# Six of 22 feed-forward convolutions in the down stage, other engines for the weight sums, and a new order at both ends of the up stage

## The chip, the cores and the metric

One core of a Trainium2 chip runs the whole program. The metric is device time in microseconds (us) from launch to end, the median of a few runs. PE is TensorE, DVE is VectorE, ACT is ScalarE, POOL is GpSimd, SP is SyncE (here it only issues DMAs).

## The reference

One layer of a diffusion trunk on 1152 tokens (128 context, 1024 latent on a 16 x 64 grid), width 1024. The part that matters is its second half, after the two token mixers:

```
h = rmsnorm(x, norm_g[2]) * (1 + sc2) + sh2
u_act, u_val = split(h @ ffn_up, 2)               # 1024 -> 2 x 2816
u_act = dwconv_grid(u_act, ffn_conv, rows) + ffn_conv_b   # 3x3 per channel
f = (silu(u_act) * u_val) @ ffn_down              # 2816 -> 1024
x = x + g2 * rmsnorm(f, norm_g[3])
```

On the grid the convolution is 3 x 3, on the 128 context tokens it has width 3. Everything is float32.

## The kernel before

A float32 matrix product is done as three reduced-precision products: an operand is split into a high part (a copy on ACT) and a low part (the difference, on DVE), and high x high, high x low and low x high are summed in PSUM. The program is one long stream for each engine. A scheduler places the instructions; where `pe.on` is set, PE keeps the order in which the code is written, and the other engines' queues are filled by the scheduler.

- **Output projection** (`wo_mm`, line 1499): nine blocks of 128 tokens. Behind each block come two norms (lines 1513 to 1525) and `modulate` (line 1466): eight transposes on PE, scale and shift on ACT and DVE, and a DMA of the normed tokens `hf` to DRAM (`h2d`). `mod_cols` computes one of eight column groups of the last gate behind each block from the second on.
- **Up stage.** The 2816 channels are 22 blocks of 128, each with an activation and a value half. The product of one block with 1152 tokens is done by Strassen's scheme in the Winograd form: the tokens are halved (c = 0, 1), and seven products P1 to P7 of sums of operand quarters take the place of eight. One product for one half of the tokens is a unit: 12 matmuls of 288 columns (line 70), so 14 units and 168 matmuls a block, 308 units in all. `w_split` (line 1614) makes the seven weight operands: ACT copies the high part (line 1622), DVE (for P5 and P3 POOL) subtracts for the low part (line 1623), and POOL forms four sums (lines 1626 to 1630). The token operands `T1` to `T4` come from `x_rest` and `x_late`.
- A unit ends in PSUM (`pu`, eight banks in a ring) and is taken out by `unit` (line 1638): P1 and P2 by ACT, then for P2 a sum on POOL (line 1658), the others by DVE (lines 1660 to 1669), into `uraw` (activation) and `uval` (value).
- `conv` (line 1671) runs one block behind: ACT writes bias and centre tap to `ua` (line 1675), DVE adds eight taps on the grid (line 47) and two on the context (line 50), ACT applies SiLU (line 1679), POOL multiplies with `uval` (line 1680) and POOL's queue sends the block to DRAM (`f2d`).
- **Down stage.** Three sweeps of three token blocks, each over k = 0 to 21. `f_group` reads `f2d` back in groups of eight k and splits it into `fg` (ACT line 1695, DVE line 1696). `wd_split` loads a row block of the down weights and splits it (ACT line 1706, DVE line 1707); `NS` = 13 of these are loaded again in each sweep, nine stay (`wr`). A sweep runs its first k over all its blocks, and the last k block by block, with the closing norm of each block behind it.

## Time and profile before

| what | value |
|---|---|
| median of three runs | 2302.42 us (2297.89 to 2305.01) |
| time of the profiled execution | 2297.62 us |
| its span, first to last instruction | 2295.9 us |
| mean granted TensorE clock | 0.961 of 2.4 GHz |
| PE / DVE / ACT / POOL busy | 90% / 65% / 38% / 37% |

In the chain of work that ended last PE has 43% of the span, DVE 27% and DMA 12%. The share of busy time is a mean over stages of very different kinds; the stretches that the change touches lie from about 1400 us on. Durations of POOL are rough, and a matmul's duration overlaps the next one's, so that matmuls are counted here from start to start.

### The profile page before, as it was taken

To read this page: it belongs to the slowest core of one execution; us is meant where nothing else is said; L and a number is where in the kernel's file an instruction comes from. 1 tells how busy PE (TensorE), PEld (TensorE's weight loads), DVE (VectorE), ACT (ScalarE), POOL (GpSimd) and SP (SyncE) were. 2 spreads that over 40 slices of the span, in tenths; PEclk is the share of its full clock that TensorE was granted. 3 is DMA by queue.
4 is the path that set the end of the run, shared out by engine and by line. 5 is a ranking of instruction groups with operands and counts; after the bars stand their busy time and mean duration, and the time that the engine had idled before them with its cause. 6 is when DMAs were issued, how large, how long until landed. Compare 5 with 4: busy or idle time off the path is not lost.

```text
span 2295.9 us, 41348 instructions
## 1 busy us (share of the span) xinstructions
PE 2062.2 (90%) x16579; PEld 1876.9 (82%) x16579; DVE 1498.9 (65%) x2219; ACT 878.6 (38%) x1702; POOL 856.5 (37%) x916
## 2 busy tenths in 40 slices
PE   5999998988999998888799997899899989779998
PEld 4998998977988887788789776888888888667787
DVE  4666779788555567545533445999999999935332
ACT  3663646362234333355311334323322322324231
POOL 2000288888432333445122011555655565200000
PEclk9999999989999999999999998999999999899999
DMA  9144444444845555467657565211221121356351
GB/s 260 52 104 113 126 126 115 130 113 120 211 109 145 137 136 140 147 201 231 227 173 244 191 191 133 67 58 58 77 68 58 58 76 59 126 182 223 121 175 46
DMA packets 401583, 305.80 MB, mean 133 GB/s; under 512 B 92369, under 2 KB 369269, under 8 KB 401392
## 3 DMA queue, kind: packets, MB, share of 16 engines
...
HBM read 220.15 MB, written 82.94 MB: 132 GB/s over the span
## 4 chain that ended last, share of the span: by engine, by line
PE 43%; DVE 27%; DMA 12%; issue 9%; ACT 6%; POOL 1%; SPq 1%; DVEq 0%; ACTq 0%; POOLq 0%
PE pg L398 10%; PE pfd L70 10%; DVE ua L47 8%; PE pwo L1499 4%; PE pbr L70 4%; PE pg L70 4%; PE pu L70 2%; DVE ua L50 2%; PE pY L70 1%; ACT ua L1675 1%; DMA aw<-in_ada_w 1%; SPq L76 1%; DMA wraw<-in_ffn_down 1%; PE pmN L70 1%; DMA bon<-bond 1%
## 5 line engine op out<-in xcount | busy, mean ns | idle before, releaser
L398 PE MATMUL pg<-act,whi 128*128 128x384 f32 (+1 forms) x1696 | 329.6, 342 | 0.9 <-DVE act L361 0.4
L70 PE MATMUL pu<-x,hl 128*128 128x288 f32 x2024 | 299.9, 298 | 30.0 <-DVE uraw L1667 27.3
L70 PEld LDWEIGHTS pu<-x,hl 128*128 128x128 f32 x2024 | 277.1, 189 | 39.1 <-issue 31.6
L398 PEld LDWEIGHTS pg<-act,whi 128*128 128x128 f32 (+1 forms) x1696 | 297.5, 189 | 7.8 <-DVE act L361 0.8
L47 DVE SCALAR_TENSOR_TENSOR ua<-uraw,par,ua 128x945 f32<-128x945 f32 (+2 forms) x176 | 253.4, 1440 | 30.9 <-ACT ua L1675 29.6
L70 PE MATMUL pu<-xb,hl 128*128 128x288 f32 x1672 | 252.1, 298 | 20.1 <-DVE uval L1662 9.1
L70 PEld LDWEIGHTS pu<-xb,hl 128*128 128x128 f32 x1672 | 231.0, 190 | 29.6 <-DVE uval L1662 13.5
L398 PE MATMUL pg<-act,wlo 128*128 128x384 f32 (+1 forms) x848 | 168.7, 338 | 8.4 <-DVE wlo L385 8.4
L70 PE MATMUL pfd<-whi,fg 128*128 128x512 f32 x468 | 150.2, 403 | 23.6 <-ACT whi L1706 13.0
L398 PEld LDWEIGHTS pg<-act,wlo 128*128 128x128 f32 (+1 forms) x848 | 147.9, 186 | 12.1 <-DVE wlo L385 8.7
L1622 ACT ACTIVATE hl<-wraw 128x512 fp32r<-128x512 f32 x132 | 79.0, 630 | 194.5 <-POOL wraw L1628 175.9
L1623 DVE TENSOR_TENSOR hl<-wraw,hl 128x512 fp32r<-128x512 f32 x110 | 135.6, 1233 | 16.6 <-ACT hl L1622 16.4
L385 DVE TENSOR_TENSOR wlo<-wraw,whi 128x1024 fp32r<-128x1024 f32 (+1 forms) x64 | 80.9, 1267 | 99.0 <-ACT whi L384 98.8
L543 POOL TENSOR_TENSOR tmp<-La,Lb 96x31 f32<-96x31 f32 (+15 forms) x155 | 124.8, 805 | 28.9 <-DMA La<-Ad 17.1
L545 POOL TENSOR_TENSOR Lb<-Lb,tmp 96x31 f32<-96x31 f32 (+15 forms) x155 | 126.8, 818 | 12.2
L70 PEld LDWEIGHTS pfd<-whi,fg 128*128 128x128 f32 x468 | 90.8, 195 | 45.2 <-ACT whi L1706 15.1
L70 PE MATMUL pfd<-wr,fg 128*128 128x512 f32 x486 | 110.6, 389 | 0.0
...
L70 PEld LDWEIGHTS pfd<-wr,fg 128*128 128x128 f32 x486 | 91.2, 188 | 18.9
L1707 DVE TENSOR_TENSOR wlo<-wraw,whi 128x1024 fp32r<-128x1024 f32 x39 | 48.0, 1231 | 87.2 <-ACT whi L1706 87.2
L70 PE MATMUL pg<-act,whi 128*128 128x384 f32 x496 | 103.3, 360 | 0.0
L1680 POOL TENSOR_TENSOR uval<-uval,ua 128x1152 f32<-128x1152 f32 x22 | 61.5, 2795 | 103.9 <-ACT ua L1679 103.9
...
## 6 DMA issues: line engine op xcount, KB each, us to landing
...
f2d<-uval POOLq DMA_DIRECT2D x22, 576.0 KB, 3.1
...
sgz<-zraw ACTq DMA_DIRECT2D x16, 576.0 KB
...
```

The costliest lines, as they stand in the source:

```text
L47: v.scalar_tensor_tensor(o, img[:, r0 + i:r1 + i, c0 + j:c1 + j], wt, o, op0=ALU.mult, op1=ALU.add)
L50: v.scalar_tensor_tensor(o, raw[:, max(0, j):128 - max(0, -j)], wt, o, op0=ALU.mult, op1=ALU.add)
L70: return (lambda *a, **k: tc.keep_in_program_order(f(*a, **k))) if self.on else f
L385: v.tensor_tensor(lo, raw, hi.bitcast(F32), op=ALU.subtract)
L398: pe.matmul(out, wt(hw, k), at(ha, k), start=(i == 0), stop=(i == last))
L543: e.tensor_tensor(t3, L[:, j, i].unsqueeze(2).to_broadcast([NI, n, m]), X[:, j:j + 1, c].to_broadcast([NI, n, m]), op=ALU.mult)
L545: e.tensor_tensor(X[:, i, c], X[:, i, c], t3, op=ALU.subtract)
L1499: pe.matmul(pts[b][q], AS[g][:, ha, k, 128 * o:128 * o + 128], wo2[k][hw][:, 0, 512 * q:512 * q + 512], start=(k == 0 and i == 0), stop=(k ...
L1622: s.activation(w[:, 0], src, AF.Copy)
L1623: (gp if m in ("P5", "P3") else v).tensor_tensor(w[:, 1], src, f32(w[:, 0]), op=ALU.subtract)
L1680: gp.tensor_tensor(val, val, ua, op=ALU.mult)
L1707: v.tensor_tensor(lo, raw, f32(hi), op=ALU.subtract)
```

## The change

- **Late convolutions.** Blocks 1, 5, 9, 13, 17 and 21 (`LATE`) have no convolution in the up stage. `put_off` sends their `uraw` and `uval` to DRAM (`latd`, on SP's queue). In the first down sweep `late_convs` loads them and runs the same convolution from new tiles (`lraw`, `lval` two each, `lua` one), three or four steps for each k. `KO` puts these six blocks at k = 16 to 21.
- **Engines.** The sum behind P2 is done by DVE straight from PSUM. All seven low parts are on DVE. Of the four weight sums two stay on POOL and two go to DVE, all four at P6.
- **Down sweeps** of 4, 3 and 2 token blocks; 15 weight blocks are loaded again in each sweep and seven stay; `f_group` has six k instead of eight.
- **Order.** `modulate` of the last token block stands behind the fourth unit, in the up products; the four first units are P1 and P2 of blocks 0 and 1 for the first half of the tokens; `x_rest(0)` and the loads of the second half stand behind it (`x_mid`, `x_late`). `mod_cols` stands behind blocks 0 to 7 instead of 1 to 8.

```
+    LATE = (1, 5, 9, 13, 17, 21)
+    KO = [i for i in range(NFB) if i not in LATE] + list(LATE)
-        (gp if m in ("P5", "P3") else v).tensor_tensor(w[:, 1], src, f32(w[:, 0]), op=ALU.subtract)
+        v.tensor_tensor(w[:, 1], src, f32(w[:, 0]), op=ALU.subtract)
-        if m == "P1":
-            gp.tensor_tensor(s1, a21, a22, op=ALU.add)
-            gp.tensor_tensor(a21, a11, a21, op=ALU.subtract)
-            gp.tensor_tensor(a11, s1, a11, op=ALU.subtract)
-        if m == "P2":
-            gp.tensor_tensor(a12, a12, a11, op=ALU.subtract)
+            gp.tensor_tensor(s1s[i], a21, a22, op=ALU.add)
+            gp.tensor_tensor(a21, a11, a21, op=ALU.subtract)
+            v.tensor_tensor(a11, s1s[i], a11, op=ALU.subtract)
+            v.tensor_tensor(a12, a12, a11, op=ALU.subtract)
...
-                s.activation(act[:, t1], pt, AF.Copy)
-                gp.tensor_tensor(act[:, t1], act[:, t1], act[:, t2], op=ALU.add)
+                v.tensor_tensor(act[:, t1], pt, act[:, t2], op=ALU.add)
...
+        def put_off(i):
+            dma(latd[LATE.index(i), 0], acts.pop(i))
+            dma(latd[LATE.index(i), 1], vals.pop(i))
+            yield
+        SWEEPS = ((0, 4), (4, 3), (7, 2))
-        NS = 13
+        NS = 15
...
+            if u == 4:
+                modulate(ob, NB - 1)
+                x_mid()
...
-                conving = conv(i)
+                conving = (put_off if i in LATE else conv)(i)
...
+        def late_convs():
+            for j, i in enumerate(LATE):
+                raw, val = (fo.tile([128, T], F32, name=nm, tag=nm) for nm in ("lraw", "lval"))
+                dma(raw, latd[j, 0])
+                dma(val, latd[j, 1])
+                yield from conv_of(i, raw, val, fd.tile([128, T], F32, name="lua", tag="lua"))
...
+                for _ in range(3 + k % 2):
+                    next(late, None)
```

PE's queue behind the last product of the output projection, before (`ptx` are transposes, `pmod` and `pmt` belong to `mod_cols`, `pu` are units):

```order
L1499 MATMUL pwo<-whi,act_164 128x512
L1473 MATMUL ptx<-ident,ob 128x128 [waits DVE_49,Activation_49]
L1473 MATMUL ptx<-ident,ob 128x128 x3
L1473 MATMUL ptx<-ident,ob 128x128 [waits PE_49]
L1473 MATMUL ptx<-ident,ob 128x128 x3
L258 MATMUL pmod<-aw,sc 32x128 [waits DMAHW3_49,Activation_49]
L258 MATMUL pmod<-aw,sc 32x128 x7
L267 MATMUL pmt<-sel,mrow 128x2 [waits Activation_49]
L70 MATMUL pu<-x_14216,hl 128x288 [waits DVE_49,Activation_49]
```

The same place of the same queue now:

```order
L1500 MATMUL pwo<-whi,act_165 128x512
L70 MATMUL pu<-x_14233,hl 128x288 [waits DVE_49]
L70 MATMUL pu<-x_14233,hl 128x288 x35
L70 MATMUL pu<-x_14233,hl 128x288 [waits Activation_49]
L70 MATMUL pu<-x_14233,hl 128x288 x7
L70 MATMUL pu<-x_14233,hl 128x288 [waits DVE_49]
L70 MATMUL pu<-x_14233,hl 128x288 x3
L70 MATMUL ptx<-ident,ob 128x128 [waits DVE_49]
L70 MATMUL ptx<-ident,ob 128x128 x7
L70 MATMUL pu<-xb_14545,hl 128x288 [waits Activation_49]
```

Four units (48 matmuls) have moved ahead of the transposes, and `mod_cols` is gone from between.

DVE's queue from the end of one up block into the next, before (`hl` are weight low parts, `ua` convolution taps, the rest takes units out of PSUM); every block reads like this:

```order
L1623 TENSOR_TENSOR hl<-wraw,hl 128x512 [waits Activation_49]
L1669 TENSOR_TENSOR uraw<-pu,uraw 128x288 [waits DVE_49,PE_49] x2
L47 SCALAR_TENSOR_TENSOR ua<-uraw,par,ua 128x15x63 [waits Activation_49]
L50 SCALAR_TENSOR_TENSOR ua<-uraw,par,ua 128x127
L47 SCALAR_TENSOR_TENSOR ua<-uraw,par,ua 128x960 [waits DVE_49]
L50 SCALAR_TENSOR_TENSOR ua<-uraw,par,ua 128x127 [waits DVE_49]
L47 SCALAR_TENSOR_TENSOR ua<-uraw,par,ua 128x15x63 [waits DVE_49]
L47 SCALAR_TENSOR_TENSOR ua<-uraw,par,ua 128x16x63 [waits DVE_49] x2
L1660 TENSOR_TENSOR uraw<-pu,uraw 128x288 [waits PE_49,Pool_49]
L1623 TENSOR_TENSOR hl<-wraw,hl 128x512 [waits DMAHW0_49,Activation_49]
```

The same place now, behind a late block (lines 1627 and 1628 are the two weight sums that came to DVE, line 1671 is the sum behind P2):

```order
L1682 TENSOR_TENSOR uraw<-pu,uraw 128x288 [waits DVE_49,PE_49]
L1633 TENSOR_TENSOR hl<-s_17934,hl 128x512 [waits Activation_49]
L1633 TENSOR_TENSOR hl<-wraw,hl 128x512 [waits PE_49,Activation_49]
L1671 TENSOR_TENSOR uraw<-pu,uraw 128x288 [waits PE_49] x2
L1633 TENSOR_TENSOR hl<-wraw,hl 128x512 [waits DMAHW0_49,Activation_49]
L1627 TENSOR_TENSOR wraw<-s_18169,wraw 128x512 [waits DVE_49,Pool_49]
L1673 TENSOR_TENSOR uraw<-pu,uraw 128x288 [waits PE_49] x2
L1633 TENSOR_TENSOR hl<-wraw,hl 128x512 [waits Activation_49]
L1628 TENSOR_TENSOR wraw<-wraw 128x512 [waits DVE_49]
```

The ten taps are gone from the block behind a late one; in the other blocks they stand between these rows as before.

ACT's queue in the first down sweep, now (`whi` and `fg` are copies of weights and of `f`, `lua` belongs to the late convolutions, line 1637 is its start and 1641 its SiLU); before, only rows like the first two kinds stood here:

```order
L1718 ACTIVATE whi<-wraw 128x1024 [waits DMAHW4_49,DVE_49,PE_49]
L1637 ACTIVATE lua<-lraw,par 128x1152 [waits DMASW4_49,DMASW5_49,DMASW3_49,DMASW6_49,DMASW2_49,DMASW7_49,DMASW1_49,DMAHW5_49,DMASW0_49,DMAHW7_49,DVE_49,Pool_49]
L1718 ACTIVATE whi<-wraw 128x1024 [waits DMAHW7_49,DVE_49,PE_49]
L1708 ACTIVATE fg<-fg 128x1024 [waits DMAHW0_49]
L1708 ACTIVATE fg<-fg 128x1024 [waits DMAHW1_49]
L1708 ACTIVATE fg<-fg 128x1024 [waits DMAHW2_49]
L1718 ACTIVATE whi<-wraw 128x1024 [waits DMAHW3_49,DVE_49,PE_49]
L1708 ACTIVATE fg<-fg 128x1024 [waits DMAHW6_49]
L1641 ACTIVATE lua<-lua 128x1152 [waits DVE_49,Activation_49]
L1718 ACTIVATE whi<-wraw 128x1024 [waits DMAHW0_49,PE_49,Activation_49]
L1637 ACTIVATE lua<-lraw,par 128x1152 [waits DMAHW4_49,Pool_49]
```

The second start of `lua` waits for POOL: there is one `lua`, and POOL's product of the convolution before it has to have read it.

## Rows read from the trace of the kernel before

**Rows 1.** Busy time of each engine by stretch (us from the span's start and length, then busy us and instructions of PE, PEld, DVE, ACT, POOL, the granted clock, the DMA share and GB/s): the head of the up stage, its steady part, the start and the rest of the down stage, the end.

```profile
1401.80:1461.20 59.40, 39.90 (x255) 37.89 (x255) 43.61 (x52) 27.69 (x47) 24.22 (x18) 0.77 0.41 94
1461.20:1982.50 521.30, 478.09 (x3470) 460.29 (x3468) 482.32 (x553) 152.00 (x262) 295.68 (x199) 1.00 0.20 64
1982.50:2102.50 120.00, 97.56 (x397) 77.30 (x397) 66.31 (x77) 48.29 (x58) 8.74 (x4) 0.90 0.57 193
2102.50:2289.90 187.40, 183.14 (x794) 149.19 (x792) 59.44 (x76) 46.22 (x69) 0.00 (x0) 0.99 0.39 133
2289.90:2295.90 6.00, 0.00 (x0) 0.00 (x0) 2.17 (x4) 0.97 (x3) 0.00 (x0) 0.68 0.23 87
```

**Rows 2.** Timeline of PE in the up stage (start, duration, engine, line, operation, count): two units that follow each other without a wait.

```profile
1462.82 1.74 PE L70 MATMUL pu<-x,hl 128*128 128x288 f32 x12
1464.40 1.75 PE L70 MATMUL pu<-xb,hl 128*128 128x288 f32 x12
```

**Rows 3.** What PE waited for in the steady up stage (total us, times, longest).

```profile
PE pu L70 <- DVE uraw L1667: 28.2, 19, 1.5
```

**Rows 4.** What DVE waited for in the same stretch.

```profile
DVE ua L47 <- ACT ua L1675: 29.0, 20, 2.0
```

**Rows 5.** Timeline of ACT, DVE and POOL around the end of one convolution and the start of the next.

```profile
1704.32 1.19 DVE L47 SCALAR_TENSOR_TENSOR ua<-uraw,par,ua 128x945 f32<-128x945 f32 x1
...
1705.60 1.17 ACT L1679 ACTIVATE ua<-ua 128x1152 f32<-128x1152 f32 x1 [3.91 <-DVE ua L47]
...
1706.85 2.69 POOL L1680 TENSOR_TENSOR uval<-uval,ua 128x1152 f32<-128x1152 f32 x1 [3.83 <-ACT ua L1679]
1707.32 2.77 DVE L1623 TENSOR_TENSOR hl<-wraw,hl 128x512 fp32r<-128x512 f32 x1 [0.48 <-ACT hl L1622]
...
1713.07 1.35 ACT L1675 ACTIVATE ua<-uraw,par 128x1152 f32<-128x1152 f32 x1 [4.74 <-DVE uraw L1669]
...
1714.45 1.38 DVE L47 SCALAR_TENSOR_TENSOR ua<-uraw,par,ua 128x945 f32<-128x945 f32 x1 [1.42 <-ACT ua L1675]
```

**Rows 6.** Groups of DVE's instructions in the steady up stage (count, busy us, mean ns of one, idle before).

```profile
L1623 DVE TENSOR_TENSOR hl<-wraw,hl 128x512 fp32r<-128x512 f32 x100 | 125.2, 1252 | 8.9 <-ACT hl L1622 8.9
...
L47 DVE SCALAR_TENSOR_TENSOR ua<-uraw,par,ua 128x960 f32<-128x960 f32 x42 | 79.8, 1900 | 0.0
...
L50 DVE SCALAR_TENSOR_TENSOR ua<-uraw,par,ua 128x127 f32<-128x127 f32 x42 | 44.0, 1047 | 0.0
```

**Rows 7.** Groups of POOL's instructions in the same stretch.

```profile
L1680 POOL TENSOR_TENSOR uval<-uval,ua 128x1152 f32<-128x1152 f32 x20 | 53.9, 2696 | 71.4 <-ACT ua L1679 71.4
...
L1627 POOL TENSOR_TENSOR wraw<-wraw 128x512 f32<-128x512 f32 x19 | 24.9, 1312 | 1.5
```

**Rows 8.** Timeline of DVE: single instructions of the kinds that an up block is made of, at a place where POOL holds none of them up.

```profile
1465.07 1.20 DVE L47 SCALAR_TENSOR_TENSOR ua<-uraw,par,ua 128x960 f32<-128x960 f32 x1
...
1466.20 0.44 DVE L1662 TENSOR_TENSOR uval<-pu,uraw 128x288 f32<-128x288 f32 x1
...
1466.57 0.67 DVE L1623 TENSOR_TENSOR hl<-wraw,hl 128x512 fp32r<-128x512 f32 x1
1467.17 1.19 DVE L47 SCALAR_TENSOR_TENSOR ua<-uraw,par,ua 128x945 f32<-128x945 f32 x1
...
1471.83 1.26 DVE L47 SCALAR_TENSOR_TENSOR ua<-uraw,par,ua 128x1008 f32<-128x1008 f32 x1
...
1473.01 0.34 DVE L50 SCALAR_TENSOR_TENSOR ua<-uraw,par,ua 128x127 f32<-128x127 f32 x1
```

**Rows 9.** Timeline of PE at the start of the up stage; in brackets the idle time ahead and what ended it.

```profile
1401.61 0.39 PE L1499 MATMUL pwo<-whi,act 128*128 128x512 f32 x1
1414.17 1.94 PE L1473 MATMUL ptx<-ident,ob 128*128 128x128 f32 x8 [12.17 <-DVE ob L1525]
...
1419.02 6.13 PE L70 MATMUL pu<-x,hl 128*128 128x288 f32 x24 [0.84 <-ACT hf L1481]
```

**Rows 10.** Timeline of PE from the up stage into the down stage, and three matmuls of the first sweep that follow each other without a wait.

```profile
1980.77 1.75 PE L70 MATMUL pu<-xb,hl 128*128 128x288 f32 x12
1991.13 0.79 PE L70 MATMUL pfd<-whi,fg 128*128 128x512 f32 x1 [8.62 <-ACT fg L1695]
1993.90 0.80 PE L70 MATMUL pfd<-whi,fg 128*128 128x512 f32 x1 [1.97 <-DVE fg L1696]
...
2026.57 1.22 PE L70 MATMUL pfd<-whi,fg 128*128 128x512 f32 x2 [9.04 <-ACT whi L1706]
...
2045.06 0.62 PE L70 MATMUL pfd<-whi,fg 128*128 128x512 f32 x2
...
2045.74 0.62 PE L70 MATMUL pfd<-whi,fg 128*128 128x512 f32 x2
```

**Rows 11.** What SP's queue waited for from 1960 us to the end (total us, times, longest).

```profile
SPq L76 <- POOL uval L1680: 11.3, 1, 11.3
```

**Rows 12.** Timeline at the start of the third down sweep: a weight load is issued, then split by ACT and DVE.

```profile
2209.93 13.04 SPq L76 DMA_DIRECT2D wraw<-in_ffn_down  x5
...
2214.19 1.06 ACT L1706 ACTIVATE whi<-wraw 128x1024 fp32r<-128x1024 f32 x1 [3.83 <-DMA wraw<-in_ffn_down]
2215.28 1.23 DVE L1707 TENSOR_TENSOR wlo<-wraw,whi 128x1024 fp32r<-128x1024 f32 x1 [3.67 <-ACT whi L1706]
```

**Rows 13.** DMA issues on the page: the finished blocks on their way to DRAM (KB each, us to landing).

```profile
f2d<-uval POOLq DMA_DIRECT2D x22, 576.0 KB, 3.1
```

More of the change, by code (lines that the diff above doesn't have):

```diff
@@ L1525, in _body @@
                 v.tensor_scalar(ob, xt, s2, None, op0=ALU.mult)
-                modulate(ob, b)
-                if b > 0:
-                    for _ in mod_cols(128 * (39 + b), 128, (8,), aw_, wt, pss):
+                if b < NB - 1:
+                    modulate(ob, b)
+                    for _ in mod_cols(128 * (40 + b), 128, (8,), aw_, wt, pss):
                         pass
@@ L1565, in x_rest, with x_mid @@
         x_split(c, "T4", td, his[3], r21)
-    x_rest(0, ta, tb, (r11, r12, r21, r22), [quarter(x2, i) for i in range(4)])
     q11, q12, q21, q22 = xb[4:8]
-    x_load(1, 0, 0, q11)
-    x_load(1, 1, 0, q21)
-    x_split(1, "X11", q11, xb[1], xb[2])
-    x_split(1, "X21", q21, xb[3], xb[8])
-    x_load(1, 0, 1, q12)
-    x_load(1, 1, 1, q22)
+    def x_mid():
+        x_load(1, 0, 0, q11)
+        x_load(1, 1, 0, q21)
+        x_split(1, "X11", q11, xb[1], xb[2])
+        x_split(1, "X21", q21, xb[3], xb[8])
+        x_rest(0, ta, tb, (r11, r12, r21, r22), [quarter(x2, i) for i in range(4)])
     def x_late():
+        x_load(1, 0, 1, q12)
+        x_load(1, 1, 1, q22)
         x_split(1, "X22", q22, xb[9], xb[10])
@@ L1777, in w_next @@
                 res[k] = wd_split(k, *(fd.tile([128, D], F32R, name=f"wr{x}{k}") for x in range(2)))
[L1779 to L1780 removed]
+        for sw, (b0, nb) in enumerate(SWEEPS):
+            pd = [[psg([128, 512], "pfd") for q in range(2)] for o in range(nb)]
             no = NFB - 3 if sw == 0 else NS
             for k in range(no):
[L1784 to L1786 removed]
+                if k in (2, 7):
+                    for _ in f_group(sw, (k + 4) // 5):
+                        pass
+                if k == 13:
+                    g3 = f_group(sw, 3)
+                    next(g3)
+                if k == no - 1:
+                    next(g3)
                 if k + 2 < NFB:
@@ L1789, in _body @@
                 w = wds.pop(k) if k < NS else res[k]
-                for o in range(3):
+                for o in range(nb):
                     for q in range(2):
                         down_mm(pd[o][q], sw, k, o, q, w, k == 0, False)
+                for _ in range(3 + k % 2):
+                    next(late, None)
+            for _ in late:
+                pass
             if sw == 0:
                 w_next(sw, NFB - 1)
-            for o in range(3):
-                b = 3 * sw + o
-                if o == 0 and sw < 2:
+            for o in range(nb):
+                b = b0 + o
+                if o == nb - 2 and sw < 2:
                     for _ in f_group(sw + 1, 0):
```

76 lines of the change are left out of this document (37 added, 39 removed).

## Prediction

> **What bounds the kernel now.** I read the busy time by stretch first, then who waits for whom in the up stage, then the timeline there, then both ends of the stage. The steady up stage takes 521.3 us for 3470 matmuls [rows 1]. A block has 168, so that is 20.65 blocks of 25.2 us. Two units that follow each other without a wait start 1.58 us apart [rows 2], so PE needs 14 x 1.58 = 22.2 us a block and stands 3 us. It waits for DVE to empty PSUM: 28.2 us in 19 waits, about one a block [rows 3]. DVE is busy 482 of 521 us, and most of the rest is the wait for ACT to begin a convolution, 29.0 us in 20 blocks [rows 4].
>
> But DVE's busy time is not work. Follow one place in the timeline [rows 5]: POOL's product runs from 1706.85 to 1709.54, a weight low part on DVE starts at 1707.32 and ends at 1710.09, 0.55 us behind it. Alone the same instruction takes 0.67 [rows 8], on the mean 1.25 [rows 6]; a 960-wide tap takes 1.20 alone and 1.90 on the mean, a context tap 0.34 and 1.05. So while POOL runs, a DVE instruction that reads two SBUF operands stands still. Instructions that take a unit out of PSUM are not held up. DVE's own work in a block, with the last 0.08 us of each duration under the next one, as the starts show [rows 8]: 5 low parts x 0.60 = 3.0; 12 PSUM reads x 0.37 = 4.4; taps 4 x 1.11 + 2 x 1.13 + 2 x 1.18 + 2 x 0.26 = 9.6 (the widths 945, 960, 1008, 127); sum 17.0. Busy is 482/20.65 = 23.4, so 6.4 us a block are held up by POOL, which is busy 295.7/20.65 = 14.3 us a block [rows 1]. The bound of the up stage is what DVE and POOL share, not DVE's arithmetic.
>
> **Steady up stage.** In a block with a convolution DVE now has 7 low parts (4.2), two weight sums priced as low parts of the same shape (1.2), 14 PSUM reads (5.2) and taps (9.6): 20.2 us. POOL keeps two weight sums (1.3 each) and the product (2.7): 5.3 us [rows 7]. With the wait for ACT, 0.8 us instead of 1.4 since a low part stands in it now, that is 21.0 us if POOL holds nothing up and 26.3 if it holds DVE up for all its length. At the old ratio (6.4 of 14.3) it is 23.4; I take 25.2, nearer the upper end, because there the product held DVE up for nearly its whole length [rows 5]. In a block behind a late one the taps and the product are gone: 10.6 us and some 2 us of POOL, 12.7.
>
> The row shows one such hold [rows 5]. The Trainium skill (SBUF — State Buffer, Who interferes with whom) makes it a rule: a VectorE instruction with two SBUF inputs and a GpSimd instruction that reads SBUF exclude each other for a whole instruction. By that rule alone POOL's 5.3 us count in full wherever DVE has no PSUM read in hand, which is rival (d), 2277 in place of 2260.
>
> Four blocks then need 3 x 25.2 + 12.7 = 88.3 us of DVE, against 4 x 22.2 = 88.8 us of PE. They tie, if DVE may fall behind by 3 us in each of three blocks and catch up in the fourth. It may: PE has eight banks, so it runs up to seven units (11 us) ahead, and the low parts stand seven or more units ahead of their use. Nine of eleven is tight, so I allow 0.6 us a block: 22.8 us. **Gain 20.65 x (25.2 - 22.8) = 50 us**, between 62 (PE's floor) and 10 (no catching up: (3 x 25.2 + 22.2)/4 = 24.4, and more if POOL holds more).
>
> The two stores of a late block go on SP's queue and wait for its last PSUM reads; queued behind them are weight loads for two blocks later, so nothing waits at once. I price them at 0.
>
> **Head of the up stage.** PE stood 12.2 us for the norm of the last token block [rows 9]. Four units, 6.3 us, now stand there. The chain of the norm itself keeps its length: in DVE's queue three low parts of operands, a difference and two PSUM reads stand between its steps, about as many as before. Also gone from PE's path are `mod_cols`, which had it from the end of the transposes at 1416.1 to 0.84 us ahead of 1419.02, and part of the slow clock: the 24 matmuls there took 6.13 us, 255 ns each [rows 9], twice the 132 ns of the steady stage [rows 2]; the mean granted clock of the stretch is 0.77, partly 1.2 and partly 2.4 GHz [rows 1]. What is late next: the operands T1 to T4 of the first half, six instructions of 1152 columns on DVE at 1.3 us (by their width, [rows 8]), stand largely behind the transposes now, and `x_late` needs the last tokens through DRAM. I expect PE to stand twice for 5 to 6 us. **Gain 9 us**, from 3 to 14.
>
> **Into the down stage.** PE stood 8.6 us, then 2.0, then ran at half speed, and stood 9.0 more at 2026.57 for a weight load [rows 10]. That load was queued on SP behind one that waited 11.3 us for the last convolution's product [rows 11]. Now the first groups of `f` are old blocks, but SP's second fetch stands behind the store of block 21, which waits for DVE, by then some 9 us behind PE. So the first wait stays near 10 to 13 us; the second goes.
>
> **First down sweep.** Two matmul pairs of it start 0.68 us apart with one more between [rows 10]: 0.227 us each. Four blocks are 528 matmuls, 119.7 us of PE. The late convolutions form a chain beside it. Between two of them: SiLU 1.2, POOL's product 2.7, the start on ACT 1.35 [rows 5] and some 0.3 of handover, 5.5 us, because there is one `lua`. Each has 9.6 us of taps, 58 in all; five gaps make 28. DVE's queue also has, between the taps of the six, 22 weight and `f` low parts of 0.9 to 1.15 [rows 12], 25 us. The first tap stands behind the weight part for k = 2, which waits for PE to finish k = 0: about 22 us after PE leaves the up stage. Behind the last tap come SiLU and product (4), the store (3.1 to landing [rows 13]), the fetch (4.3, as a weight load takes from issue to use [rows 12]) and the split (2.3): 14 us. So k = 20 and 21 are ready 22 + 58 + 28 + 25 + 14 = 147 us after the up stage, and PE, which could be there at 125, waits; then 69 matmuls, half of the first ones slow, take 19 us. **The sweep ends 167 us after the up stage**, between 140 (chain hidden) and 180.
>
> The one or two weight parts in each gap may stand under POOL's product as the one at 1707.32 did [rows 5], some 6 us in all; that is kept for the range.
>
> **Other sweeps.** The second has 396 matmuls, 90 us, and 1 us of switch. The third has 264, 60 us, but only 2.7 us a k. A weight load takes 4.3 us from issue to use and 2.3 us to split [rows 12], 6.6 for one of two buffers, 3.3 a k: 11 of the 15 loaded k cost 0.6 more, 6 us. At two blocks a sweep this is a new wait for DMA. So from the up stage's end to the last matmul 167 + 91 + 66 = 324 us, against 1982.5 to 2289.9 = 307.4 before [rows 1]. **Loss 17 us**, from a gain of 10 to a loss of 30. The 6 us behind the last matmul stay.
>
> **Sum.** -50 - 9 + 17 = -42 us on the profiled 2297.6; the median shown is 4.8 higher, so 2302.4 - 42, rounded to 2260.
>
> **Rivals.** (a) The chain of late convolutions hides behind PE, as its DVE work of some 100 us in 120 would allow: the sweep takes 140, the rest as above: 2233, at PE's floor in the up stage 2221. Against it stands the one `lua`. (b) The late blocks don't help, because three blocks in a row with a convolution already fill the banks: 24.4 to 25 us a block, gain 10 instead of 50: 2300. For it speaks that PE already waits for PSUM in every block [rows 3]. (c) Slower: weights, convolution inputs and `f` share SP's queue in the first sweep. An input two convolutions on waits for POOL's product, weights stand behind it, and taps stand behind their low parts on DVE. If the loop closes, each late convolution costs a load and a split more (4.3 + 2.3): 6 x 6.6 = 40 us. It decides from the point where a weight load is issued less than 6.6 us before its low part is due; by my times the margin is 1 to 8 us. With (b) it gives 2340, alone 2300. (d) POOL holds DVE up for all its 5.3 us: 26.3 us a block, 13.2 behind a late one, 92.1 us for four, 23.0 a block and 0.6 as above, gain 33 instead of 50: 2277. For it speaks the hold at 1707.32 [rows 5], against it that PSUM reads are a quarter of DVE's work and run beside POOL. With (b) this is 25.3 a block, no gain in the up stage at all, so the change would not do there what it says: 2311.
>
> **How the numbers follow.** Forecast (2240 to 2285) 0.50; (a) 0.15; (b) 0.13; (c) 0.10; (d) 0.12. The measurement can tell 0.3%, 7 us, from no change. Faster: forecast, (a), (d) and a small part of (b) and (c): 0.79; same 0.09; slower 0.12. The range 2228 to 2296 leaves out the lower end of (a) and most of (b) and (c).
>
> **What the next profile would show.** Right: blocks of 22 to 23.5 us in the up stage; low parts near 0.8 us on the mean instead of 1.25; POOL busy near 5 us a block; a wait of 15 to 30 us of PE in the first sweep before k = 20, ended by `fg`; weights awaited by ACT in the third. Wrong: PE still waiting for PSUM in every block, no wait in the first sweep, or many waits there for `whi` and `wlo` behind loads.

## The result and the profile after

The changed kernel takes 2265.72 us (median of four runs, 2261.67 to 2274.78) against 2302.61 us before (four runs too): a ratio of 0.9848, 95% interval 0.981 to 0.9885. 2260 was forecast, in a range of 2228 to 2296.

The profiled execution of the changed kernel is its slowest, 2274.78 us, and was slow ahead of everything that the change touches: the output projection begins at 1289.3 us there and at 1278.5 in the profile of before, and in the twelve profiles below, whose code up to that point is the same, between 1279.3 and 1291.6. So stages are compared, not spans. From the first matmul of the output projection to the end it is 1017.4 us before and 983.5 after, 33.9 less; the medians say 36.9.

The view by stretch of the changed kernel (columns as in [rows 1]): from the end of the output projection through the first three up blocks, the last 19 up blocks, from there to the end of the first down sweep, the second sweep, the third.

```profile
1415.10:1511.30 96.20, 75.98 (x513) 74.81 (x514) 75.30 (x111) 36.32 (x55) 16.03 (x10) 0.88 0.33 88
1511.30:1932.70 421.40, 421.40 (x3193) 421.18 (x3192) 396.19 (x579) 124.35 (x197) 109.14 (x65) 1.00 0.24 78
1932.70:2098.00 165.30, 126.25 (x530) 100.54 (x530) 115.06 (x123) 61.63 (x70) 23.43 (x14) 0.91 0.59 217
2098.00:2193.40 95.40, 92.18 (x398) 73.74 (x397) 34.77 (x44) 26.82 (x38) 0.00 (x0) 1.00 0.49 165
2193.40:2266.60 73.20, 65.51 (x265) 50.82 (x263) 26.50 (x33) 21.62 (x31) 0.00 (x0) 0.95 0.40 132
```

The same view of the kernel before, its last 19 up blocks:

```profile
1497.70:1982.50 484.80, 441.59 (x3194) 423.79 (x3192) 447.84 (x513) 140.64 (x244) 276.41 (x187) 1.00 0.20 64
```

19 blocks took 484.8 us, 25.5 each; they take 421.4, 22.2 each, and PE is busy for all of it: it waits for nothing there where it waited once a block [rows 3]. POOL went from 276.4 us to 109.1. Groups of DVE's instructions in that stretch of the changed kernel (columns as in [rows 6]):

```profile
L1633 DVE TENSOR_TENSOR hl<-wraw,hl 128x512 fp32r<-128x512 f32 x109 | 105.5, 968 | 0.0
L50 DVE SCALAR_TENSOR_TENSOR ua<-uraw,par,ua 128x127 f32<-128x127 f32 x30 | 24.6, 822 | 0.0
```

A low part takes 968 ns on the mean, 1252 before [rows 6], still more than the 670 of one that is not held up [rows 8].

The head gained nothing, 96.2 us against 95.7 in before's trace:

```profile
1402.00:1497.70 95.70, 76.20 (x532) 74.39 (x532) 78.08 (x92) 38.86 (x63) 43.48 (x30) 0.86 0.33 81
```

Timeline of the changed kernel there, PE's waits and what stood behind the longest:

```profile
1417.10 8.16 PE L70 MATMUL pu<-x,hl 128*128 128x288 f32 x48 [2.01 <-DVE ob L1517]
...
1431.95 1.97 PE L70 MATMUL ptx<-ident,ob 128*128 128x128 f32 x8 [6.69 <-DVE ob L1526]
...
1442.48 0.55 SPq L76 DMA_DIRECT2D h2d<-hf  x1
...
1445.71 1.69 POOL L1625 TENSOR_TENSOR s<-wraw 128x512 f32<-128x512 f32 x1 [64.23 <-DMA h2d<-hf]
...
1448.77 1.36 ACT L1632 ACTIVATE hl<-wraw 128x512 fp32r<-128x512 f32 x2 [1.33 <-POOL wraw L1626]
...
1450.17 12.30 PE L70 MATMUL pu<-x,hl 128*128 128x288 f32 x72 [9.28 <-ACT hl L1632]
```

PE's 12.2 us in one piece [rows 9] became 2.0, 6.7 and 9.3. The last is new. In the change both halves of the last block's normed tokens go through the one buffer `hf` (before, the second half had another). The weight sum `s` is written into this buffer too, and the second half is being stored from it until 1445.7; the split that PE waits for needs what is derived from `s`.

The down stage. What PE waited for from the up stage to the end in the changed kernel (total us, times, longest):

```profile
PE pfd L70 <- ACT fg L1708: 31.3, 2, 24.2
PE pfd L70 <- DVE wlo L1719: 8.1, 12, 1.7
PE pfd L70 <- ACT whi L1718: 7.1, 6, 2.8
```

And its timeline in the first sweep, from one late convolution to the next, and from the last one to the matmul that needs it:

```profile
1984.18 1.20 DVE L47 SCALAR_TENSOR_TENSOR lua<-lraw,par,lua 128x945 f32<-128x945 f32 x1
...
1985.42 1.17 ACT L1641 ACTIVATE lua<-lua 128x1152 f32<-128x1152 f32 x1 [1.13 <-DVE lua L47]
...
1986.67 2.66 POOL L1642 TENSOR_TENSOR lval<-lval,lua 128x1152 f32<-128x1152 f32 x1 [14.26 <-ACT lua L1641]
...
1989.37 1.35 ACT L1637 ACTIVATE lua<-lraw,par 128x1152 f32<-128x1152 f32 x1 [2.78 <-POOL lval L1642]
...
1990.75 1.20 DVE L47 SCALAR_TENSOR_TENSOR lua<-lraw,par,lua 128x945 f32<-128x945 f32 x1 [4.23 <-ACT lua L1637]
...
2067.81 1.16 ACT L1641 ACTIVATE lua<-lua 128x1152 f32<-128x1152 f32 x1 [10.23 <-DVE lua L47]
2069.06 2.60 POOL L1642 TENSOR_TENSOR lval<-lval,lua 128x1152 f32<-128x1152 f32 x1 [15.43 <-ACT lua L1641]
...
2078.76 1.06 ACT L1708 ACTIVATE fg<-fg 128x1024 fp32r<-128x1024 f32 x1 [9.79 <-DMA fg<-f2d]
...
2079.87 0.79 PE L70 MATMUL pfd<-wr,fg 128*128 128x512 f32 x1 [24.20 <-ACT fg L1708]
```

Between these two convolutions lie 5.4 us (1985.38, the tap's end, to 1990.75); the five gaps are 5.4, 5.4, 5.4, 6.8 and 7.4 us, 30 in all. And `f` of the last two blocks is ready 147.2 us after the up stage's end at 1932.7. PE waits 24.2 us for it.

So against before: output projection +2.2, head +0.5, the last 19 up blocks -63.4, from the up stage through the first sweep +45.0 (four blocks instead of three), second sweep -0.8, third -17.6 (two instead of three), tail +0.2: -33.9.

### The profile page after: what moved, and what is told of

Same layout as the page of the kernel before. It is cut to its first block, busy times and chain, and to the rows that moved or that the text cites. A ratio compares the mean times of both kernels' runs of the same rounds, so it can differ in the third digit from the quotient of the medians.

```text
span 2272.9 us, 41306 instructions
## 1 busy us (share of the span) xinstructions
PE 2059.0 (91%) x16579; PEld 1883.0 (83%) x16579; DVE 1500.1 (66%) x2355; ACT 875.3 (39%) x1662; POOL 677.5 (30%) x784
## 4 chain that ended last, share of the span: by engine, by line
PE 49%; DMA 15%; POOL 12%; DVE 12%; issue 5%; ACT 5%; SPq 1%; ACTq 0%; POOLq 0%; DVEq 0%
PE pu L70 18%; PE pg L399 6%; POOL Lb L546 5%; POOL tmp L544 5%; PE pfd L70 5%; PE pwo L1500 4%; PE pbr L70 4%; PE pg L70 3%; DMA wraw<-in_ffn_down 2%; DVE lua L47 2%; DMA aw<-in_ada_w 1%; DMA La<-Ad 1%; PE pY L70 1%; DVE ua L47 1%; DMA bon<-bond 1%
## 5 line engine op out<-in xcount | busy, mean ns | idle before, releaser
L70 PE MATMUL pu<-xb,hl 128*128 128x288 f32 x1672 | 247.3, 295 | 2.2 <-DVE xb L1456 1.4
L70 PE MATMUL pfd<-whi,fg 128*128 128x512 f32 x540 | 171.4, 399 | 14.7 <-ACT whi L1718 7.1
L47 DVE SCALAR_TENSOR_TENSOR ua<-uraw,par,ua 128x945 f32<-128x945 f32 (+2 forms) x128 | 161.7, 1263 | 11.0 <-ACT ua L1637 11.0
L386 DVE TENSOR_TENSOR wlo<-wraw,whi 128x1024 fp32r<-128x1024 f32 (+1 forms) x64 | 80.9, 1267 | 96.4 <-ACT whi L385 96.3
L70 PEld LDWEIGHTS pfd<-whi,fg 128*128 128x128 f32 x540 | 103.0, 192 | 39.4 <-ACT whi L1718 10.1
L546 POOL TENSOR_TENSOR Lb<-Lb,tmp 96x31 f32<-96x31 f32 (+15 forms) x155 | 128.5, 829 | 12.1
L1633 DVE TENSOR_TENSOR hl<-wraw,hl 128x512 fp32r<-128x512 f32 x132 | 124.4, 943 | 2.0 <-ACT hl L1632 2.0
L70 PE MATMUL pfd<-wlo,fg 128*128 128x512 f32 x270 | 108.7, 403 | 8.4 <-DVE wlo L1719 8.1
L70 PE MATMUL pfd<-wr,fg 128*128 128x512 f32 x378 | 88.6, 395 | 26.9 <-ACT fg L1708 24.2
L1642 POOL TENSOR_TENSOR uval<-uval,ua 128x1152 f32<-128x1152 f32 x16 | 44.5, 2782 | 214.9 <-ACT ua L1641 214.9
L70 PEld LDWEIGHTS pfd<-wr,fg 128*128 128x128 f32 x378 | 71.7, 190 | 43.4 <-ACT fg L1708 24.6
L1500 PE MATMUL pwo<-whi,act 128*128 128x512 f32 x288 | 95.7, 410 | 4.0 <-ACT whi L385 4.0
```

The lines of the kernel that those rows point to most:

```text
L47: v.scalar_tensor_tensor(o, img[:, r0 + i:r1 + i, c0 + j:c1 + j], wt, o, op0=ALU.mult, op1=ALU.add)
L70: return (lambda *a, **k: tc.keep_in_program_order(f(*a, **k))) if self.on else f
L386: v.tensor_tensor(lo, raw, hi.bitcast(F32), op=ALU.subtract)
L546: e.tensor_tensor(X[:, i, c], X[:, i, c], t3, op=ALU.subtract)
L1500: pe.matmul(pts[b][q], AS[g][:, ha, k, 128 * o:128 * o + 128], wo2[k][hw][:, 0, 512 * q:512 * q + 512], start=(k == 0 and i == 0), stop=(k ...
L1633: v.tensor_tensor(w[:, 1], src, f32(w[:, 0]), op=ALU.subtract)
```

## The experiments

Each kernel is the changed one with the edit shown, except before_no_pool. Stages, in us, come from the one profile of each kernel; the ratio is to the kernel before on the same chip, and since the chips differ, kernels are compared by it. "Head" runs from the end of the output projection to the end of the third up block, "19 up" are the blocks behind it, "sweep 1" begins with the up stage's end. A sweep is compared only among kernels with the same number of blocks in it.

| kernel | head | 19 up | sweep 1 | sweep 2 | sweep 3 | ratio (95%) |
|---|---|---|---|---|---|---|
| before (3, 3, 3 blocks) | 95.7 | 484.8 | 120.3 | 96.2 | 90.8 | 1 |
| changed (4, 3, 2) | 96.2 | 421.5 | 165.3 | 95.4 | 73.2 | 0.985 (0.981 to 0.989) |
| late_off | 94.1 | 464.9 | 134.8 | 95.5 | 71.5 | 0.991 (0.988 to 0.994) |
| pool_back | 98.3 | 441.1 | 169.1 | 98.4 | 71.1 | 0.994 (0.992 to 0.997) |
| late_off_pool_back | 101.2 | 485.9 | 138.4 | 96.6 | 74.6 | 1.003 (1.001 to 1.005) |
| two_lua | 96.2 | 421.5 | 151.1 | 94.1 | 71.6 | 0.978 (0.974 to 0.981) |
| hf_own | 89.0 | 421.5 | 168.3 | 95.6 | 71.4 | 0.983 (0.980 to 0.986) |
| raw_own | 96.1 | 421.5 | 167.4 | 89.8 | 64.4 | 0.980 (0.977 to 0.983) |
| late5 | 96.3 | 427.0 | 144.5 | 95.0 | 71.8 | 0.977 (0.974 to 0.980) |
| all5 | 89.1 | 426.9 | 136.6 | 92.6 | 63.2 | 0.967 (0.964 to 0.969) |
| no_pool_off | 91.5 | 427.7 | 132.4 | 92.9 | 74.0 | 0.971 (0.969 to 0.972) |
| all5_prod | 88.4 | 421.5 | 136.3 | 92.4 | 63.9 | 0.964 (0.962 to 0.965) |
| before_no_pool (3, 3, 3) | 95.8 | 435.6 | 111.2 | 94.5 | 92.1 | 0.975 (0.973 to 0.977) |
| best | 89.4 | 423.1 | 134.0 | 91.0 | 64.4 | 0.964 (0.961 to 0.966) |

### What brought the up stage to PE's pace: late convolutions, or less on POOL?

**late_off.**

```
-    LATE = (1, 5, 9, 13, 17, 21)
+    LATE = ()
```

> All convolutions are back in the up stage (the list of late ones is empty); who sums and subtracts, the head and the sweeps of 4, 3, 2 blocks stay as in the changed kernel. Theory A (putting off every fourth convolution is what brought the up stage to PE's 22.2 us a block, since four blocks of VectorE work then fit beside four of PE): VectorE was busy 448.7 us in 21.27 blocks of the changed kernel's trace, 21.1 us a block; a quarter of the 9.6 us of taps comes back, 23.5 us, and with what POOL holds up to the 25.2 us of before. Up stage 25 to 58 us longer over 19 blocks; the first down sweep, without the chain of late convolutions, 131 to 140 us instead of 165.3. Together 2257 to 2297 us. Theory B (moving the sums off POOL did it alone): the up stage stays at 22.2 to 22.6 us a block and only the sweep changes: 2232 to 2240 us.

2285.4 us. The last 19 up blocks of this kernel by stretch, and what PE waited for in them:

```profile
1504.20:1969.00 464.80, 432.95 (x3193) 427.76 (x3192) 449.98 (x629) 130.51 (x207) 124.80 (x74) 0.99 0.21 67
```

```profile
PE pu L70 <- DVE uraw L1680: 31.9, 19, 2.2
```

24.5 us a block, and one wait for PSUM in each is back: theory A by its number, 43 us more in the up stage and 30 less in the first sweep. It also prices a block with its convolution by itself.

**pool_back.**

```
-            v.tensor_tensor(a11, s1s[i], a11, op=ALU.subtract)
-            v.tensor_tensor(a12, a12, a11, op=ALU.subtract)
+            gp.tensor_tensor(a11, s1s[i], a11, op=ALU.subtract)
+            gp.tensor_tensor(a12, a12, a11, op=ALU.subtract)
...
-        v.tensor_tensor(w[:, 1], src, f32(w[:, 0]), op=ALU.subtract)
+        (gp if m in ("P5", "P3") else v).tensor_tensor(w[:, 1], src, f32(w[:, 0]), op=ALU.subtract)
...
-                v.tensor_tensor(act[:, t1], pt, act[:, t2], op=ALU.add)
+                s.activation(act[:, t1], pt, AF.Copy)
+                gp.tensor_tensor(act[:, t1], act[:, t1], act[:, t2], op=ALU.add)
```

> The two weight sums, the low parts of P5 and P3 and the sum after P2 are back on POOL (P2's eviction on ACT again) as in the kernel before; the late convolutions, the head and the sweeps stay as in the changed kernel. Theory A (late convolutions alone suffice): VectorE has 23.4 us a block with POOL's hold as before, less a quarter of a convolution (9.6 us of taps and what POOL holds them up), some 20.5 to 21 us, under PE's 22.2: up stage at 22.2 to 22.5 us a block, 2262 to 2272 us. Theory B (the hold of POOL had to go too: three blocks in a row with a convolution run at 23.4 to 25.2 us and fill the banks): 23 to 24 us a block, 15 to 35 us more, 2281 to 2301 us.

2293.3 us. By stretch, the last 19 up blocks:

```profile
1503.70:1944.80 441.10, 426.92 (x3194) 421.65 (x3192) 392.24 (x468) 132.92 (x234) 257.41 (x176) 1.00 0.23 74
```

Theory A falls: 23.2 us a block, theory B's number. Two of four blocks take 22.2 us and two 24 to 25 (1525.9, 1548.1, 1573.0, 1597.7, 1619.9 are the starts of five that follow each other). Late convolutions alone don't reach PE's pace.

**late_off_pool_back**, both edits:

> No late convolutions and the sums back on POOL: of the change only the head and the sweeps of 4, 3, 2 blocks are left. Theory A (the two parts are worth 43 us and 20 us in the up stage on their own and meet PE's floor together): the up stage is back at 25.5 us a block, 485 us over its last 19 blocks, the down stage at the 308 us that it takes without late convolutions against 313 before: 2297 to 2305 us. Theory B (head or sweeps carry a gain or a loss of their own of 10 us or more): under 2292 or over 2312 us.

2313.9 us against 2305.8 before on its chip. The up blocks are back at 485.9 us, as theory A has it. The two parts bring 21.0 us (485.9 to 464.9, engines alone) and 44.8 us (485.9 to 441.1, late convolutions alone), together 64.4: they add up but for 1.4 us, where PE's pace ends it. The total is above theory A's range. The head takes 101.2 us, 5.5 more than before, and from the up stage's end to the end of the program it is 315.9 us where theory A had 308. With the old work on POOL the new order of the head is a loss, and the new sweeps gain nothing (309.6 us for the three, 307.3 before).

**late5**, every fifth convolution put off, with the two buffers of two_lua below:

```
-    LATE = (1, 5, 9, 13, 17, 21)
+    LATE = (1, 6, 11, 16, 21)
```

> The kernel with two buffers for the late sums, and every fifth convolution put off instead of every fourth: five of them. Theory A (a block with its convolution takes 24.5 us when nothing is put off, one without some 13, so five blocks need 111 us where PE needs 110.9): the up stage stays at 22.2 to 22.4 us a block; the chain in the first sweep is one convolution of 16 us shorter, so the wait of 11.0 us that two buffers left goes: 2241 to 2247 us. Theory B (four convolutions in a row fill the PSUM banks before the put-off block can make up for them): 22.6 to 23 us a block, 8 to 16 us more: 2250 to 2262 us.

2256.7 us, nothing gained on two_lua. The chain's wait went (first sweep 144.5 instead of 151.1), and the up stage gave it back: 427.0 us, where one block in five takes 24 us and the others 22.2. That is 22.5 us a block, between the two theories; the total lies in theory B's range, and its mechanism is there: PE waits for PSUM three times, up to 1.7 us.

### What POOL's work costs VectorE

**no_pool_off.** As late_off, and with it:

```
-            gp.tensor_tensor(s1s[i], a21, a22, op=ALU.add)
-            gp.tensor_tensor(a21, a11, a21, op=ALU.subtract)
+            v.tensor_tensor(s1s[i], a21, a22, op=ALU.add)
+            v.tensor_tensor(a21, a11, a21, op=ALU.subtract)
...
-        gp.tensor_tensor(val, val, ua, op=ALU.mult)
+        yield
+        v.tensor_tensor(val, val, ua, op=ALU.mult)
```

> All convolutions in the up stage, as in the run without late ones (24.5 us a block there), and nothing left on POOL but the issue of stores: the product of each convolution and the two weight sums that were still there run on VectorE. Theory A (a VectorE instruction beside one of POOL lasts until POOL is done, 3.5 us a block by the instructions' excess over their usual length; on VectorE the product costs 1.3 us and the two sums 0.6 us each): 24.5 - 3.5 + 2.5 = 23.4 to 23.6 us a block, 16 to 20 us off the up stage: 2262 to 2270 us. Theory B (the long instructions are no cost of POOL's, and the work only moves onto the engine that is the bound): 26.5 to 27 us a block, 40 to 48 us more: 2325 to 2335 us.

2238.9 us: VectorE, the engine that bounds the stage, got all that POOL still did, and the 19 blocks went from 464.9 to 427.7 us. Groups of DVE's instructions in these blocks, of late_off:

```profile
L47 DVE SCALAR_TENSOR_TENSOR ua<-uraw,par,ua 128x945 f32<-128x945 f32 (+2 forms) x154 | 194.7, 1265 | 14.8 <-ACT ua L1637 14.8
L1633 DVE TENSOR_TENSOR hl<-wraw,hl 128x512 fp32r<-128x512 f32 x112 | 117.6, 1051 | 0.0
L50 DVE SCALAR_TENSOR_TENSOR ua<-uraw,par,ua 128x127 f32<-128x127 f32 x38 | 27.4, 720 | 0.0
```

and of no_pool_off:

```profile
L47 DVE SCALAR_TENSOR_TENSOR ua<-uraw,par,ua 128x945 f32<-128x945 f32 (+2 forms) x152 | 183.6, 1208 | 0.7 <-ACT ua L1637 0.7
L1633 DVE TENSOR_TENSOR hl<-wraw,hl 128x512 fp32r<-128x512 f32 x112 | 75.7, 676 | 0.0
L1643 DVE TENSOR_TENSOR uval<-uval,ua 128x1152 f32<-128x1152 f32 x19 | 25.5, 1344 | 0.0
...
L1625 DVE TENSOR_TENSOR s<-wraw 128x512 f32<-128x512 f32 x19 | 12.9, 677 | 0.0
...
L50 DVE SCALAR_TENSOR_TENSOR ua<-uraw,par,ua 128x127 f32<-128x127 f32 x38 | 12.8, 337 | 0.0
```

With POOL empty, low parts and context taps have their undisturbed length (676 and 337 ns, [rows 8]). The three groups are shorter by 11.1, 41.9 and 14.6 us, 67.6 in all or 3.6 a block, as theory A has it (2.5 us of this are two taps more in late_off's stretch, so the hold is some 65); the work that came costs 25.5 and twice 12.9. The 19 blocks of no_pool_off by stretch:

```profile
1507.50:1935.20 427.70, 424.83 (x3194) 421.04 (x3192) 426.98 (x681) 134.32 (x207) 10.15 (x19) 1.00 0.22 72
```

VectorE's busy time fell by 23.0 us (449.98 to 426.98), a little more than theory A's 16 to 20. What theory A left out is the idle time ahead of the first tap, 14.8 us and now 0.7: other work of VectorE stands in that gap. So it sized the gain at half, and the total is 23 us below its range.

**before_no_pool.** The kernel before, with this alone:

```
-        (gp if m in ("P5", "P3") else v).tensor_tensor(w[:, 1], src, f32(w[:, 0]), op=ALU.subtract)
+        v.tensor_tensor(w[:, 1], src, f32(w[:, 0]), op=ALU.subtract)
...
-            gp.tensor_tensor(s1, a21, a22, op=ALU.add)
+            v.tensor_tensor(s1, a21, a22, op=ALU.add)
...
-                s.activation(act[:, t1], pt, AF.Copy)
-                gp.tensor_tensor(act[:, t1], act[:, t1], act[:, t2], op=ALU.add)
+                v.tensor_tensor(act[:, t1], pt, act[:, t2], op=ALU.add)
...
-            gp.tensor_tensor(val, val, ua, op=ALU.mult)
+            yield
+            v.tensor_tensor(val, val, ua, op=ALU.mult)
```

(and the other three weight sums in the same way).

> The kernel before, with nothing else changed than that the feed-forward's up stage leaves POOL nothing but the issue of stores: weight sums, low parts, the sum after P2 and the convolution's product run on VectorE. Theory A (of the change's gain in the up stage the cause is POOL's hold on VectorE, and late convolutions only make up for what is left of it): the 22.6 us a block that were measured with all convolutions in place and POOL empty, against 25.5 before, over 19 blocks 55 us less: 2244 to 2252 us, below the changed kernel. Theory B (the new head and the new sweeps are needed for it, or the work is too much in the old order): 23.5 us a block or more, 2263 us or more.

2247.1 us, less than the changed kernel. By stretch, its last 19 up blocks:

```profile
1504.30:1940.00 435.70, 429.29 (x3194) 422.21 (x3192) 427.36 (x680) 137.40 (x205) 10.12 (x19) 1.00 0.22 70
```

22.9 us a block, 0.3 above theory A's, and its total holds. No late convolution, new head or other sweeps is needed for three quarters of what the up stage gained (49.2 us of 63.3). Against no_pool_off, which has the new order and the new sweeps without late convolutions, the up blocks take 7.9 us more (435.6 for 427.7) and the head 4.3 more, but the three sweeps together take as long (297.8 and 299.3): sweeps of 4, 3 and 2 blocks alone bring nothing.

### The waits in the first sweep, in the head and in the later sweeps

**two_lua.**

```
-                yield from conv_of(i, raw, val, fd.tile([128, T], F32, name="lua", tag="lua"))
+                yield from conv_of(i, raw, val, fo.tile([128, T], F32, name="lua", tag="lua"))
...
-                x = fo.tile([128, D], F32, name="x", tag="x")
+                x = fo.tile([128, T], F32, name="x", tag="lraw")[:, 0:D]
...
-                ob = fo.tile([128, D], F32, name="ob", tag="ob")
+                ob = fo.tile([128, T], F32, name="ob", tag="lval")[:, 0:D]
```

> Two buffers for the convolution's sum in the down stage instead of one (the output blocks take the buffers of the late convolutions afterwards, to make room). Theory A (the chain of late convolutions is late because VectorE stands between two of them while SiLU, product and the next scaling go through the one buffer, 5.3 us from one convolution's last tap to the next one's first, five times): the last group is ready 120 to 127 us after the up stage instead of 147, PE's wait of 24.2 us before it falls to 0 to 4 us, the first sweep takes 141 to 145 us instead of 165.3: 2242 to 2246 us. Theory B (the chain is paced by something else: its steps stand behind weight splits that wait for PE to free a buffer, or behind fetches): the wait shrinks by less than 10 us, 2256 to 2266 us.

2253.2 us, between the theories. PE's wait of 24.2 us fell to 11.0:

```profile
PE pfd L70 <- ACT fg L1708: 18.0, 2, 11.0
```

The first sweep by stretch, and in the timeline the fourth product beside VectorE's taps:

```profile
1922.90:2074.00 151.10, 127.55 (x529) 102.43 (x530) 126.52 (x124) 62.14 (x71) 33.00 (x14) 0.92 0.67 237
```

```profile
2010.69 6.37 POOL L1642 TENSOR_TENSOR lval<-lval,lua 128x1152 f32<-128x1152 f32 x1 [14.42 <-ACT lua L1641]
...
2011.94 0.34 DVE L50 SCALAR_TENSOR_TENSOR lua<-lraw,par,lua 128x127 f32<-128x127 f32 x1
2012.21 1.19 DVE L47 SCALAR_TENSOR_TENSOR lua<-lraw,par,lua 128x945 f32<-128x945 f32 x1
2013.32 1.21 DVE L1719 TENSOR_TENSOR wlo<-wraw,whi 128x1024 fp32r<-128x1024 f32 x1
2014.45 3.62 DVE L47 SCALAR_TENSOR_TENSOR lua<-lraw,par,lua 128x960 f32<-128x960 f32 x1
```

The five gaps, 30 us, are gone; but with one `lua` VectorE had stood while POOL multiplied, and with two they run at once and hold each other: the product takes 6.37 us instead of 2.66, a tap 3.62 instead of 1.2. VectorE is busy 126.5 us with the 124 instructions of this stretch, 115.1 with 123 in the changed kernel: 11.4 us of the gain went there. The last product, behind which PE waits, takes 6.0 us instead of 2.6, which costs 3.4 more.

**hf_own.**

```
-            if q == 0 or b == NB - 1:
+            if b == NB - 1:
+                hf = cv.tile([128, T], F32, name="hf", tag="uval")[:, 0:512].rearrange("p (j t) -> p j t", t=128)
+            elif q == 0:
...
```

> The two halves of the last block's modulated rows go into buffers of their own instead of the one that the weight sums use. Theory A (in the head the wait of 9.3 us for a split of weights comes from that buffer: the second half waits for the first half's store, and POOL's sum for the second's): PE's wait of 9.3 us goes, what comes after is bound by VectorE (75 to 90 per cent busy there), so 4 to 9 us are gained: 2257 to 2262 us. Theory B (VectorE's splits of the input's second part, not the buffer, set the head): PE waits as long a few units later, gain 0 to 3 us, 2263 to 2266 us.

2267.1 us; the ratio of 0.983 can't be told from the changed kernel's 0.985, though the head can: 89.0 us instead of 96.2. What PE waited for there:

```profile
PE ptx L70 <- DVE ob L1528: 6.1, 1, 6.1
PE pu L70 <- DVE ob L1519: 3.0, 1, 3.0
PE pu L70 <- DVE xb L1456: 2.5, 1, 2.5
```

The 9.3 us for `hl` are gone; theory A holds for the stage, and its total lies 5 us above the range.

**raw_own**, with `x` and `ob` placed as in two_lua:

```
-            raw = wp.tile([128, D], F32, name="wraw", tag="wlo", bufs=4)
+            raw = rawp[0].tile([128, D], F32, name="wraw", tag=rawp[1], bufs=rawp[2])
...
         res = {}
+        rawp[:] = [fo, "draw", 2]
```

> In the down stage the fetched rows of the weights go into two buffers of their own; before they shared four with the low parts (the output blocks take the late convolutions' buffers, to make room). One late buffer `lua`, as in the changed kernel. Theory A (in the sweep of two blocks PE waits because a row and a low part each hold one of four buffers until PE is done, so a pair of steps takes 6.6 us where PE needs 5.4): the third sweep takes 62 to 66 us instead of 73.2, the second 91 to 94 instead of 95.4, together 2253 to 2258 us. Theory B (the bytes come no faster, or the fetches stand in SP's queue behind the load of an output block): the third sweep stays at 70 us or more, 2262 to 2267 us.

2261.6 us. The third sweep by stretch:

```profile
2183.30:2247.70 64.40, 62.31 (x264) 48.18 (x263) 26.50 (x33) 21.33 (x31) 0.00 (x0) 1.00 0.42 143
```

Theory A for the sweeps: 64.4 us instead of 73.2 (71.1 to 74.6 in the kernels of the table whose rows share the buffers, the combined ones aside), and the second 89.8 instead of 95.4, PE's own: 396 matmuls of 0.2267 us, from the three in 0.68 us of [rows 10]. It was the buffers, not the bytes. In the third sweep PE's idle time went from 7.7 to 2.1 us and its busy time from 65.5 to 62.3. The second part is the clock: granted 0.95 on the mean in the changed kernel, with 6.8 us at 1.2 GHz and the rest at 2.4, in two stretches that begin right behind PE's waits of 1.7 and 2.8 us for `whi`; now it is 1.00. The total is above theory A's range, since the first sweep took 167.4 us; by ratio it is 11 us under the changed kernel, with intervals that overlap by a little.

### Together

**all5.** late5, hf_own and raw_own, and in the first sweep each product on VectorE behind the next convolution's start:

```
+                s.activation(ua, raw, AF.Identity, scale=P("ffn_conv", 22 * 4 + i), bias=P("ffn_conv_b", i))
+                yield
+                if prev:
+                    v.tensor_tensor(prev[1], prev[1], prev[2], op=ALU.mult)
+                    pdma(f2d[KO.index(prev[0])], prev[1])
...
```

> Everything that helped or should help, together: every fifth convolution put off, two buffers for the late sums with the late product on VectorE, the last norm's halves in buffers of their own, the fetched rows of the down weights in buffers of their own. Theory A (the parts lie in different stages and add up: 13 us for two buffers, 10 for the fifth, 7 for the head, 10 for the rows): 2224 to 2232 us. Theory B (they meet in the first down sweep, or the up stage leaves PE's floor): 2236 to 2248 us.

2231.5 us, the upper end of theory A's range. Head and third sweep gain what they gained singly (89.1 and 63.2 us), the second sweep half of it (92.6). The 10 us for the fifth convolution did not come: the up stage is off PE's pace as in late5 (426.9 us), which is theory B's condition. The first sweep makes up for it, 136.6 us for 144.5 in late5. That the late product on VectorE did this is likely, but it was not run by itself.

**all5_prod**, the product of the up stage on VectorE as well (the edit of no_pool_off, without its sums):

> The kernel with everything together, and the product of each convolution in the up stage on VectorE as well (the two weight sums stay on POOL). Theory A (POOL's product holds one VectorE instruction for 2.1 us a block, VectorE does it in 1.3): the four blocks with convolutions out of five come under 23.9 us each, the up stage is back at PE's floor of 22.2 us a block, 5 to 6 us less: 2224 to 2228 us. Theory B (VectorE is the bound and gets more work): 22.7 to 23 us a block, 5 to 10 us more: 2236 to 2242 us.

2221.7 us, 3.6% under the kernel before and 2 us below theory A's range. The last 19 up blocks are at PE's pace again (421.5 us), as theory A has it.

**best**, all5_prod with the two sums on VectorE too, and two late blocks instead of five:

```
+    LATE = (10, 21)
```

> The kernel with everything together, the two weight sums on VectorE too, and only two convolutions put off, those of blocks 10 and 21. Theory A (with POOL empty a block takes 22.6 us on VectorE, 0.4 more than PE; the PSUM banks and one block without taps in the middle take that up, and the last block's convolution no longer stands ahead of the down stage; a chain of two ends long before the first sweep needs it): up stage at 22.2 us a block, first sweep 126 to 131 us instead of 136: 2211 to 2217 us. Theory B (0.4 us a block are not taken up over ten blocks): 4 to 8 us more in the up stage, 2218 to 2224 us, no better than five put off.

2221.9 us, no better: theory B's number, for another reason. The up stage is 1.6 us above PE's pace, but the down stage starts 10.6 us late:

```profile
PE pfd L70 <- DVE uraw L1685: 10.6, 1, 10.6
```

VectorE, busy 416.4 of 423.0 us in the 19 blocks, is that far behind PE when the products end, and putting off block 21 doesn't change it: in no_pool_off, which puts off none, the down stage starts 10.2 us late. In all5_prod, where VectorE has slack (395.2 of 421.5), it is 4.2 us.

## Why the prediction was right, step by step

- **The bound and the cause.** That DVE and POOL share the bound, and that DVE's length beside POOL is not work, was right and is now shown both ways: with POOL empty low parts take 676 ns. At what share POOL counts was left between nothing and all, and taken at 4.2 us of hold for 5.3 us of POOL a block, 0.8. In late_off it is some 65 us of hold for 124.8 us of POOL, 3.4 for 6.6 a block or 0.52: POOL was busy longer than forecast (its second weight sum takes 2.08 us, not 1.3, and 0.6 us a block go to issuing the store) and held DVE up for less of it, so two errors partly cancel: with the prediction's 20.2 and 0.8 us, 3.4 gives 24.4. Rival (d), all of it, falls: the blocks that it put at 26.3 us take 24.5.
- **Steady up stage.** The mechanism is right, the term too small. 25.2 us for a block with a convolution is 24.5 (late_off), so with the forecast's 12.7 for a late one (not measured by itself) three and a late one need 86 us, less than four blocks of PE, and the allowance of 0.6 us was not used: 22.2, not 22.8. The forecast's 2.4 us a block were 3.3. Rival (b), full banks, falls; a milder form of it is what happens when POOL keeps its work (pool_back, 23.2 us a block for its 24.4 to 25).
- **The two stores at 0.** Right: PE waits for nothing in the 19 blocks.
- **Head.** The step that failed: 9 us were to be gained, none was. "Twice for 5 to 6 us" left out a buffer: `hf` is also the buffer of the weight sum, and the second half of the last norm's store holds it. hf_own gives 7.2 us of the 9. Nor did the slow clock go: granted 0.86 on the mean in this stretch before, 0.88 now.
- **Into the down stage.** 7.1 us, then no second wait of 9: somewhat better than the 10 to 13.
- **First sweep.** Right: 165.3 us for 167, the wait of 24.2 within 15 to 30, the last group ready at 147.2 for 147, three of the five gaps 5.4 for 5.5. That 147 is met to 0.2 us is luck: the first tap starts at 19.3 us and not 22, from it to the last tap's end it is 115.7 us and not 111, and 12.1 and not 14 follow. Rivals (a) and (c) fall. two_lua shows that the one buffer is the cause of the gaps, and that nearly half of what they cost (11.4 and 3.4 of 30 us) comes back as hold.
- **Other sweeps.** The mechanism (a buffer pair takes 6.6 us) is right and the size is not: 95.4 and 73.2 us for 91 and 66. The second sweep was priced without a wait, though it took 96.2 us in the kernel before already: PE waits there for `whi` and `wlo`, 3.8 us before and 3.1 in the changed kernel. In the third PE's clock falls behind the waits. Buffers for the fetched rows take both away (raw_own).
- **Sum.** -42 forecast, -33.9 in the profiles from the output projection on, -36.9 in the medians. The up stage was better by 4 us in all (head and blocks together: -62.9 for -59), the down stage worse by 10 (+26.8 for +17), and the output projection 2 us longer (its length varies from 123.0 to 126.5 us over the profiles). That 2260 was met so closely is luck in part. The stretch of the head as measured here has 1.65 of the forecast's 20.65 blocks in it, so for it -13 was forecast and +0.5 measured, for the 19 blocks -46 and -63.4, and behind them +17 and +26.8: errors of some 13, -17 and 10 us.

The Trainium skill (Perfetto Trace Analysis, Optimizing Scalar/DVE Operations) says that moving operations between VectorE and GpSimd might not help, since they share a port. Here the row is sharper: such a move had made it worse, and taking all of it back is worth 49 us (before_no_pool).
